# Twenty seven-product pairs instead of eighteen in a down projection, with two weight sums joined into one instruction

## The chip, the cores and the metric

The kernel runs on one core of a Trainium2 chip. The metric is the device time of one execution in microseconds (us). Three runs of the kernel before took 1113.10 to 1113.37 us, median 1113.29. One more execution was profiled; all durations and waits below come from it.

## The reference

One layer of a streaming encoder for 256 tokens of width 2048, in float32: a joint input projection, eight heads of retention beside eight heads of latent attention, an output projection, a layer norm, a feed-forward block, a second layer norm. What matters here is the feed-forward block, whose second product is the down projection:

```python
x = _layer_norm(DEEPNORM_ALPHA * x + mix, ln1_g[l], ln1_b[l])
h = jnp.square(jax.nn.relu(x @ w_up[l])) @ w_down[l]      # 256x2048 @ 2048x8192, then 256x8192 @ 8192x2048
x = _layer_norm(DEEPNORM_ALPHA * x + h, ln2_g[l], ln2_b[l])
```

## The kernel before, in words

**Precision by splitting.** TensorE multiplies in a reduced float32 (fp32r). Each operand is therefore split into a rounded high half (a cast on ScalarE, line 388) and the remainder, its low half (a subtraction on VectorE, line 389). A product is three matmuls: high by high, high by low, low by high.

**The down projection.** It has two passes (`p`), one for each half of the 2048 output columns. A pass runs over 32 pairs of 128-row blocks of `w_down`. A pair is one load of 1 MB into one of three raw buffers (`raw_wd`, DMA issued on SP's queue), and is then cut into pieces: a piece is a high and a low half of 1024 columns, in one of five rotating slots (`hi_wd`, `lo_wd`). ScalarE can write a piece only when TensorE is done with the piece that held the slot before. `ORDER` says in which order a pass takes the activation blocks; in pass 1 the first ten positions take weight pairs 28 to 31 and 22 to 27 and then 0, 1, 2 and on, so that the tile `lo_wd1_26` belongs to position 8 and `lo_wd1_0` to position 10. Before every second position a block of activations is split too (`r_split`, a cast and the subtraction of line 1011, tile `rhl`), except for the first positions of pass 1, whose blocks are still there. The last four pairs of pass 1 are kept for the end. The sums of a pass lie in PSUM banks (`d`).

**Ordinary and seven-product pairs.** An ordinary pair (`pair_products`) has two pieces and 24 matmuls of 512 columns. A seven-product pair (`seven_products`) takes the two by two blocks of the pair's product and forms them from seven block products in place of eight (Winograd's form of Strassen's scheme): 7 x 3 = 21 matmuls, into the banks `d` and four more (`s`). For that VectorE makes sums first. Of the activations there are four (`token_sums`, lines 363 to 366, 128 columns each, then a cast on ScalarE and a remainder on VectorE, line 368). Of the weight blocks b11, b12, b21, b22 there are four as well (`weight_sums`, lines 398 to 401, 512 columns each): t1 = b12 - b11, t3 = b22 - b12, then b12 becomes b22 - t1, then t4 = b21 - b12. t1 and t3 lie side by side in one tile, `t13`. Then four pieces are split, three of 1024 columns and one of 512: the two rows of the pair, `t13`, and t4 (tile `ut`). The table `SEVEN` names the positions of a pass that are seven-product pairs; 9 in each pass before. The up projection has 20 such pairs of its own, and the change doesn't touch their number. After the last seven-product pair of a pass the four extra banks are added into the result (`add_sums`), in between the pairs that follow, and at the start of pass 1 pass 0's banks are added to the residual.

**What sets the order.** The program is written out by hand; each engine runs its instructions in the order in which they are emitted. Pieces are emitted ahead of their use: after every part of a pair's matmuls, `unit()` emits up to two further pieces if the slots allow it, and the side work that waits. So VectorE's order (which sums, which low half, which split comes next) is fixed when the kernel is built, and moves when `SEVEN` moves.

**The end.** The last layer norm is written out in blocks of 512 columns. `shifted` finishes a block of the second 128 tokens on VectorE and writes it from SP's queue; one block is finished on ScalarE and written from ScalarE's queue. The last two writes are 384 and 128 columns.

Of the kernel before, what the change touches and what calls it, by code (L numbers as in the profile page):

```python
# [14 lines left out]
P = 128  # L15
# [19 lines left out]


ORDER = (tuple(range(16)), (14, 15, 11, 12, 13) + tuple(range(11)))
SEVEN = ((4, 7, 10, 12, 15, 18, 21, 24, 27), (2, 4, 7, 9, 12, 14, 17, 19, 22))


UP_PAIRS = (3, 5, 6)
UP_SEVEN = ((), (3, 5)) + 6 * (UP_PAIRS,)
# [37 lines left out]
def kernel(  # L80
# [19 lines left out]
    nc = tc.nc  # L100
# [60 lines left out]
    def raw_tile(job, name):  # L161
        job.raw = wraw.tile([P, 2048], F32, tag="raw", name=name)
        return job.raw
# [172 lines left out]
    for half in range(2):  # L336
        row = []
        for i in range(KT // 2):
            kp = (i + H // 2) % (KT // 2)
            n = i - (KT // 2 - 3)  # L340
            row.append(weights(w_out[half, kp], 2048, f"wo{half}{kp}",
                               into=staged_out(n) if half and n >= 0 else None))
# [15 lines left out]
    extra = {}  # L358
# [8 lines left out]
        nc.scalar.copy(v[:, :, 0], st)  # L367
        return lambda: nc.vector.tensor_sub(v[:, :, 1], st, v[:, :, 0].bitcast(F32))

    def weights_pair(name, load, half, sums=None, seven=False, into=None):  # L370


        job = Job(None, [], into is None or None in into)

        def shaped(t, like):
            return t if len(like.shape) == 2 else t.rearrange("p (f c) -> p f c", c=P)

        def split(i, src, n=1024):
            if into is None or into[i] is None:
                hi = wsp.tile([P, 1024], F32R, tag="hi", name=f"hi_{name}_{i}")  # L380
                lo = wsp.tile([P, 1024], F32R, tag="lo", name=f"lo_{name}_{i}")
            else:
                o = into[i] * 2048
                hi, lo = extra["sx"][:, o:o + 1024], extra["sx"][:, o + 1024:o + 2048]
            job.hi.append(hi)
            job.lo.append(lo)
            h, l = shaped(hi[:, 0:n], src), shaped(lo[:, 0:n], src)
            nc.scalar.copy(h, src)  # L388
            nc.vector.tensor_sub(l, src, h.bitcast(F32))  # L389

        def first_sums():
            job.rest = sums()

        def weight_sums():

            b11, b12, b21, b22 = (half(job, e, 4 * j, 4 * j + 4) for e in range(2) for j in range(2))
            t1, t3, t4 = (shaped(t, b11) for t in (extra["t13"][:, 0:512], extra["t13"][:, 512:], extra["t4"]))
            nc.vector.tensor_sub(t1, b12, b11)
            nc.vector.tensor_sub(t3, b22, b12)
            nc.vector.tensor_sub(b12, b22, t1)  # L400
            nc.vector.tensor_sub(t4, b21, b12)
            if sums:
                job.rest()

        job.load = lambda: load(job)
        if not seven:
            job.pieces = [lambda e=e: split(e, half(job, e, 0, 8)) for e in range(2)]
            job.loose = 0 if into is None else 2 - into.count(None)
        else:
            job.pieces = ([first_sums] if sums else []) + [weight_sums]  # L410
            job.loose = len(job.pieces)
            job.pieces += [lambda: split(0, half(job, 1, 0, 8)), lambda: split(1, half(job, 0, 0, 8)),
                           lambda: split(2, extra["t13"]), lambda: split(3, extra["t4"], 512)]
        job.free = [[False] for _ in job.pieces[job.loose:]]
        jobs.append(job)
        return job

    def up_pair(b, kp):
        def load(job):
            raw = raw_tile(job, f"raw_wu{b}_{kp}")  # L420
            nc.sync.dma_start(raw.rearrange("p (f c) -> p f c", f=8),
                              w_up[8 * b:8 * b + 8, :, kp * 256:(kp + 1) * 256].rearrange("f p c -> p f c"))

        def half(job, e, i, j):
            return job.raw.rearrange("p (f e c) -> p f e c", f=8, e=2)[:, i:j, e]

        return weights_pair(f"wu{b}_{kp}", load, half, None, kp in UP_SEVEN[b])

    def down_pair(p, pair, into=None, seven=None):
        def load(job):  # L430
            raw = raw_tile(job, f"raw_wd{p}_{pair}")
            nc.sync.dma_start(raw.rearrange("p (e c) -> p e c", e=2),
                              w_down[2 * pair:2 * pair + 2, :, p * 1024:(p + 1) * 1024].rearrange("e p c -> p e c"))

        def half(job, e, i, j):
            return job.raw[:, e * 1024 + i * P:e * 1024 + j * P]

        def sums():
            k = 2 * pair
            r0, r1 = (rr[k // 32][:, k % 32 + e] for e in range(2))  # L440
            st = spare_flat[:, seven * 512:(seven + 1) * 512].rearrange("p (i c) -> p i c", i=4)
            return token_sums(r0, r1, st, sums_of(seven))

        return weights_pair(f"wd{p}_{pair}", load, half, None if seven is None else sums, seven is not None, into)

    def sums_view(t):
        return t.rearrange("p (i h c) -> p i h c", i=4, h=2)
# [1 line left out]
    def sums_of(q):  # L449
        return sums_view(extra["sx"][:, q * 1024:(q + 1) * 1024])  # L450
# [14 lines left out]
    for p in range(2):  # L465
        for n, pair in enumerate(pairs[p]):
            if p == 0 or n < 32 - NHELD:
                j_down[p][pair] = down_pair(p, pair, None, SEVEN[p].index(n) % 2 if n in SEVEN[p] else None)
                if p == 1 and n == STAGE_AT:
                    pair = pairs[1][32 - NHELD]  # L470
                    j_down[1][pair] = down_pair(1, pair, (2, 3))
            elif n > 32 - NHELD:
                j_down[p][pair] = down_pair(p, pair, (1, None) if n == 33 - NHELD else None)
    j_down[0][pairs[0][SEVEN[0][0]]].held = True
    row_job(2, [])
# [544 lines left out]
    for i in range(2):  # L1020
        t = work.tile([P, 2048], F32R, tag="big", name=f"us{i}", bufs=2)
# [114 lines left out]
    for b in range(1, 8):  # L1136
# [3 lines left out]
        for n in range(8):  # L1140
            job = j_block[b][n]
# [15 lines left out]
    extra["sx"] = slab.tile([P, 8192], F32R, tag="slab", name="sx")  # L1157
    j_down[0][pairs[0][SEVEN[0][0]]].held = False
    st2 = [stat.tile([P, 4, 6], F32, tag=f"ln{tb}", name=f"lm{tb}", bufs=1) for tb in range(2)]
    u, v = spare_flat[:, 0:512], spare_flat[:, 512:]  # L1160
# [44 lines left out]
    for p in range(2):  # L1205
        cb = [[(acc, bank)[p](f"d{p}{tb}{j}") for j in range(2)] for tb in range(2)]
        mb = None
        for n, pair in enumerate(pairs[p][:32 if p == 0 else 32 - NHELD]):
            b = pair // 2
            if n % 2 == 0:  # L1210
# [5 lines left out]
                if p == 1 and n == STAGE_AT:  # L1216
                    r_split(ORDER[1][15], -1)
            if n in SEVEN[p]:
                if mb is None:
                    mb = [(bank, acc)[p](f"s{p}{j}") for j in range(4)]  # L1220
                seven_products(j_down[p][pair], rhls[b], pair % 2 * 2, sums_of(SEVEN[p].index(n) % 2), cb, mb,
                               n == SEVEN[p][0], n == SEVEN[p][-1])
                if n == SEVEN[p][-1]:
# [57 lines left out]
    nc.tensor.matmul(last, scaled, col(1, 2), start=False, stop=False)  # L1281
    nc.tensor.matmul(last, warm, g2[:, 1024:1536], start=False, stop=True)

    def shifted(j, a, b):
        cs = slice(j * 512 + a, j * 512 + b)
        c = xt[:, 1, cs]
        nc.vector.scalar_tensor_tensor(c, c, rss[1], b2[:, cs], op0=ALU.mult, op1=ALU.add)
        nc.sync.dma_start(out[P:2 * P, cs], c)

    centred(1, 3, cb[1][1])  # L1290
    centred(1, 0, col(1, 0))
    shifted(3, 0, 512)
    shifted(0, 0, 512)
    nc.scalar.copy(col(1, 2), last)
    nc.scalar.dma_start(out[P:2 * P, 1024:1536], col(1, 2))
    centred(1, 1, col(1, 1))
    shifted(1, 0, 384)
    shifted(1, 384, 512)


# [77 lines left out]
```

## Time and profile before

| what | us |
|---|---|
| median of three runs | 1113.29 |
| the profiled execution: its time | 1114.0 |
| the profiled execution: its span, first to last instruction | 1111.9 |
| TensorE (PE) busy | 1103.4 |
| VectorE (DVE) busy | 903.6 |
| ScalarE (ACT) busy | 611.5 |

The runs in the table are without the profiler; the profiled execution's time is 2.1 us more than its span, for what lies around it. Rows of instructions in the profile name the engine, the line of the kernel, the operation, the tile written and the tiles read, with shapes. Rows by time begin with the start and the duration in us; "x2" merges two that follow each other, and what stands in brackets is the idle time before the row and the engine that ended it. Rows of waits name who waited for whom, then the us in total, how many times, and the longest. Rows by stage give each engine's busy us in a stretch of the span. Weight loads of the array (PEld) overlap matmuls. The granted TensorE clock was 1.00 in every stage of the down projection.

### The profile page before, as it was taken

What the parts mean: (1) busy time and instruction counts of PE and PEld (TensorE: products, weight loads), DVE (VectorE), ACT (ScalarE), POOL (GpSimd) and SP (SyncE); (2) the same over time, 40 slices, a digit from 0 to 9 for tenths busy, and PEclk for the clock granted to TensorE, in tenths of its full rate; (3) what the DMA queues carried; (4) which work ended last, traced back from release to release, by engine and by line L of the source; (5) the groups of instructions that cost most, each with busy time, mean ns of one, the idle gap of its engine ahead of it and who ended that gap; (6) DMA issues with size and microseconds to landing.
All of it is one profiled execution on the core that took longest, in us unless ns stands there. A gap on an engine that the chain in (4) does not pass through costs nothing.

```text
span 1111.9 us, 13691 instructions
## 1 busy us (share of the span) xinstructions
PE 1103.4 (99%) x5196; PEld 921.7 (83%) x5196; DVE 903.6 (81%) x1253; ACT 611.5 (55%) x793; POOL 9.6 (1%) x18
## 2 busy tenths in 40 slices
PE   9999999999999999999999999999999999999997
PEld 8888888888888889888888888888888888888875
DVE  6676784666665777899998999899999998999986
ACT  4445664535453456355666656746765664566650
POOL 0000000000000000000000000000000000000000
PEclk9999999999999999999999999999999999999999
DMA  8655364444465544566656756655656665656672
GB/s 306 224 205 189 119 233 178 154 159 161 150 259 195 200 190 151 191 224 207 212 176 202 226 153 200 217 176 171 220 187 213 206 222 175 209 190 198 206 253 100
DMA packets 92561, 217.09 MB, mean 195 GB/s; under 512 B 4176, under 2 KB 62544, under 8 KB 84432
## 3 DMA queue, kind: packets, MB, share of 16 engines
q1 hardware_dynamic: 92208, 215.70, 57.5%
q8 instruction: 40, 0.66, 0.3%
q10 hardware_dynamic: 288, 0.52, 0.1%
q14 instruction: 25, 0.20, 0.1%
HBM read 214.12 MB, written 2.10 MB: 194 GB/s over the span
## 4 chain that ended last, share of the span: by engine, by line
PE 97%; DVE 1%; DMA 1%; issue 0%; ACT 0%; POOL 0%; SPq 0%; DVEq 0%
PE d L301 22%; PE u L301 18%; PE r L301 16%; PE o L301 8%; PE v L1079 5%; PE m L301 5%; PE s L1079 4%; PE u L1079 4%; PE d L1079 3%; PE up L723 2%; PE pu L723 2%; PE ut L1126 1%; PE pv L301 1%; PE up L729 1%; DMA raw_mla<-in_w_mla 1%; PE pu L729 1%
## 5 line engine op out<-in xcount | busy, mean ns | idle before, releaser
L388 ACT CAST hi_wu<-raw_wu 128x1024 fp32r<-128x1024 f32 x112 | 118.2, 1059 | 117.9 <-DVE raw_wu L400 60.4
L388 ACT CAST hi_wd<-raw_wd 128x1024 fp32r<-128x1024 f32 x125 | 130.3, 1053 | 63.6 <-PE d L301 32.8
L389 DVE TENSOR_TENSOR lo_wd<-raw_wd,hi_wd 128x1024 fp32r<-128x1024 f32 x125 | 148.6, 1219 | 18.2 <-ACT hi_wd L388 17.0
L301 PE MATMUL u<-hi_wu,x1hl 128*128 128x512 f32 x576 | 162.7, 393 | 0.0
L301 PE MATMUL d<-hi_wd,rhl 128*128 128x512 f32 x568 | 156.5, 390 | 0.0
L389 DVE TENSOR_TENSOR lo_wu<-raw_wu,hi_wu 128x1024 fp32r<-128x1024 f32 x112 | 133.2, 1219 | 22.3 <-ACT hi_wu L388 21.6
L301 PE MATMUL r<-hi_ret,xhl 128*128 128x512 f32 x512 | 147.0, 397 | 0.0
L301 PEld LDWEIGHTS d<-hi_wd,rhl 128*128 128x128 f32 x568 | 106.3, 188 | 21.9
L301 PEld LDWEIGHTS u<-hi_wu,x1hl 128*128 128x128 f32 x576 | 106.3, 188 | 21.0
L301 PEld LDWEIGHTS r<-hi_ret,xhl 128*128 128x128 f32 x512 | 93.9, 188 | 18.2
L190 DVE TENSOR_TENSOR lo_ret<-raw_ret,hi_ret 128x1024 fp32r<-128x1024 f32 x64 | 75.7, 1220 | 23.9 <-ACT hi_ret L189 23.7
L301 PE MATMUL u<-lo_wu,x1hl 128*128 128x512 f32 x288 | 89.0, 390 | 0.0
L301 PE MATMUL d<-lo_wd,rhl 128*128 128x512 f32 x284 | 87.9, 390 | 0.7 <-DVE lo_wd L389 0.7
L301 PE MATMUL r<-lo_ret,xhl 128*128 128x512 f32 x256 | 79.4, 391 | 0.0
L189 ACT CAST hi_ret<-raw_ret 128x1024 fp32r<-128x1024 f32 x64 | 64.9, 1051 | 16.3 <-PE r L301 12.2
L301 PEld LDWEIGHTS u<-lo_wu,x1hl 128*128 128x128 f32 x288 | 54.0, 188 | 11.4
L301 PEld LDWEIGHTS d<-lo_wd,rhl 128*128 128x128 f32 x284 | 53.2, 188 | 12.2 <-DVE lo_wd L389 1.1
L301 PE MATMUL o<-hi_wo,mix 128*128 128x512 f32 x208 | 57.1, 392 | 0.0
L301 PEld LDWEIGHTS r<-lo_ret,xhl 128*128 128x128 f32 x256 | 48.0, 188 | 10.4
L190 DVE TENSOR_TENSOR lo_wo<-raw_wo,hi_wo 128x1024 fp32r<-128x1024 f32 x26 | 31.2, 1222 | 19.6 <-ACT hi_wo L189 18.9
L301 PEld LDWEIGHTS o<-hi_wo,mix 128*128 128x128 f32 x208 | 38.7, 188 | 7.8
L301 PE MATMUL m<-hi_mla,xhl 128*128 128x512 f32 (+1 forms) x168 | 42.5, 363 | 0.0
(299 smaller groups left out, 1978.2 us busy)
## 6 DMA issues: line engine op xcount, KB each, us to landing
raw_wu<-in_w_up SPq DMA_DIRECT2D x64, 1024.0 KB, 5.7
raw_wd<-in_w_down SPq DMA_DIRECT2D x64, 1024.0 KB, 5.6
raw_ret<-in_w_ret SPq DMA_DIRECT2D x32, 1024.0 KB, 4.8
raw_wo<-in_w_out SPq DMA_DIRECT2D x16, 1024.0 KB, 4.8
raw_mla<-in_w_mla SPq DMA_DIRECT2D x14, 672.0 KB, 5.2
raw_qk<-in_w_qk SPq DMA_DIRECT2D x8, 640.0 KB, 3.9
row<-in_ln_rows SPq DMA_DIRECT2D x4, 1024.0 KB, 5.9
raw_uv<-in_w_uv SPq DMA_DIRECT2D x2, 1024.0 KB, 4.9
```

The lines of the kernel that those rows point to most:

```text
L189: nc.scalar.copy(hi[:, o:e], r)
L190: nc.vector.tensor_sub(lo[:, o:e], r, hi[:, o:e].bitcast(F32))
L301: nc.tensor.matmul(accs[j][:, :w], x_part, w_part[:, a:a + w], start=first and fst and i == 0, stop=last and lst and i == len(steps) - 1)
L388: nc.scalar.copy(h, src)
L389: nc.vector.tensor_sub(l, src, h.bitcast(F32))
L723: nc.tensor.matmul(pb, hi[:, a:a + P], hl[:, k0 + i], start=first and i == ks[0], stop=last and i == ks[-1])
L729: nc.tensor.matmul(pb[:, 0:S], lo[:, a:a + P], hl[:, k0 + i, 0:S], start=False, stop=last and i == ks[-1])
L1079: nc.tensor.matmul(pb, x_part, w_part, start=alone and first and fst, stop=alone and last and lst)
L1126: nc.tensor.transpose(pts[i][:, f * P:(f + 1) * P], gathered[i][:, f * P:(f + 1) * P], ident)
```

## The change

Three edits. First, `weight_sums` makes t1 and t3 in one subtraction of 1024 columns: `columns` gives the views [b12, b22] and [b11, b12] of the raw weights, and their difference fills `t13`. This holds for every seven-product pair, in the up projection too. Second, `SEVEN` names ten positions in each pass, at other places. Third, the very last write of 128 columns is issued from ScalarE's queue. What is computed stays the same but for rounding. Lines from 427 on are up to 9 further down.

```diff
-SEVEN = ((4, 7, 10, 12, 15, 18, 21, 24, 27), (2, 4, 7, 9, 12, 14, 17, 19, 22))
+SEVEN = ((4, 6, 9, 11, 14, 16, 19, 22, 24, 27), (2, 4, 6, 8, 10, 12, 14, 17, 19, 22))
...
-            t1, t3, t4 = (shaped(t, b11) for t in (extra["t13"][:, 0:512], extra["t13"][:, 512:], extra["t4"]))
-            nc.vector.tensor_sub(t1, b12, b11)
-            nc.vector.tensor_sub(t3, b22, b12)
+            t1, t4 = (shaped(t, b11) for t in (extra["t13"][:, 0:512], extra["t4"]))
+            second, first, t13 = columns(job, extra["t13"])
+            nc.vector.tensor_sub(t13, second, first)
             nc.vector.tensor_sub(b12, b22, t1)
             nc.vector.tensor_sub(t4, b21, b12)
...
+        def columns(job, t):
+            v = job.raw.rearrange("p (f e c) -> p f e c", f=8, e=2)
+            return (v[:, 4:8].rearrange("p f e c -> p e f c"), v[:, :, 0].rearrange("p (j f) c -> p j f c", j=2),
+                    t.rearrange("p (j f c) -> p j f c", j=2, c=P))
...
+        def columns(job, t):
+            return (job.raw.rearrange("p (e j c) -> p e j c", e=2, j=2)[:, :, 1],
+                    job.raw[:, 0:1024].rearrange("p (j c) -> p j c", j=2), t.rearrange("p (j c) -> p j c", j=2))
...
-    def shifted(j, a, b):
+    def shifted(j, a, b, queue=nc.sync):
...
-        nc.sync.dma_start(out[P:2 * P, cs], c)
+        queue.dma_start(out[P:2 * P, cs], c)
...
-    shifted(1, 384, 512)
+    shifted(1, 384, 512, nc.scalar)
```

On VectorE, the sums of weight pair 2 in pass 1 (position 12, a seven-product pair in both programs), before:

```order
L366 TENSOR_TENSOR xm_2766<-rr0_3643,xm_2766 128x128
L398 TENSOR_TENSOR t13_3672<-raw_wd1_2_8067 128x512
L399 TENSOR_TENSOR t13_3672<-raw_wd1_2_8067 128x512
L400 TENSOR_TENSOR raw_wd1_2_8067<-raw_wd1_2_8067,t13_3672 128x512
L401 TENSOR_TENSOR ut_3645<-raw_wd1_2_8067 128x512
L368 TENSOR_TENSOR sx_6382<-xm_2766,sx_6382 128x4x128
```

and now:

```order
L366 TENSOR_TENSOR xm_2766<-rr0_3643,xm_2766 128x128
L399 TENSOR_TENSOR t13_3672<-raw_wd1_2_8030 128x1024
L400 TENSOR_TENSOR raw_wd1_2_8030<-raw_wd1_2_8030,t13_3672 128x512
L401 TENSOR_TENSOR ut_3645<-raw_wd1_2_8030 128x512
L368 TENSOR_TENSOR sx_6362<-xm_2766,sx_6362 128x4x128
```

Lines 398 and 399 have become one instruction of 1024 columns.

On VectorE again, from position 9 to position 10 of pass 1 (`lo_wd1_27` to `lo_wd1_0`; `xm` holds the token sums, `rhl` is a split of activations). Before, position 9 is a seven-product pair and 10 an ordinary one:

```order
L389 TENSOR_TENSOR lo_wd1_27_2_8033<-t13_3672,hi_wd1_27_2_8032 128x1024
L1011 TENSOR_TENSOR rhl_8036<-rr0_3643,rhl_8036 128x4x256
L389 TENSOR_TENSOR lo_wd1_27_3_8052<-ut_3645,hi_wd1_27_3_8051 128x512
L389 TENSOR_TENSOR lo_wd1_0_0_8070<-raw_wd1_0_7981,hi_wd1_0_0_8069 128x1024
L389 TENSOR_TENSOR lo_wd1_0_1_8080<-raw_wd1_0_7981,hi_wd1_0_1_8079 128x1024
```

and now position 9 is ordinary, and 10 has sums of its own:

```order
L389 TENSOR_TENSOR lo_wd1_27_0_8014<-raw_wd1_27_7929,hi_wd1_27_0_8013 128x1024
L1020 TENSOR_TENSOR rhl_8017<-rr0_3643,rhl_8017 128x4x256
L389 TENSOR_TENSOR lo_wd1_27_1_8027<-raw_wd1_27_7929,hi_wd1_27_1_8026 128x1024
L363 TENSOR_TENSOR xm_2766<-rr0_3643 128x128
L364 TENSOR_TENSOR xm_2766<-xm_2766,rr0_3643 128x128
L365 TENSOR_TENSOR xm_2766<-rr0_3643 128x128
L366 TENSOR_TENSOR xm_2766<-rr0_3643,xm_2766 128x128
L399 TENSOR_TENSOR t13_3672<-raw_wd1_0_7945 128x1024
L400 TENSOR_TENSOR raw_wd1_0_7945<-raw_wd1_0_7945,t13_3672 128x512
L401 TENSOR_TENSOR ut_3645<-raw_wd1_0_7945 128x512
L368 TENSOR_TENSOR sx_6362<-xm_2766,sx_6362 128x4x128
L389 TENSOR_TENSOR lo_wd1_0_0_8048<-raw_wd1_0_7945,hi_wd1_0_0_8047 128x1024
```

One split of activations stands between the first low half of position 8 and that of position 10; between position 4 and 6, and 6 and 8, there is none, and between 10 and 12, and 12 and 14, one each.

More of the change, by code (lines that the diff above doesn't have):

```diff
@@ L368, in token_sums, with weights_pair @@
         return lambda: nc.vector.tensor_sub(v[:, :, 1], st, v[:, :, 0].bitcast(F32))
-    def weights_pair(name, load, half, sums=None, seven=False, into=None):
+    def weights_pair(name, load, half, columns, sums=None, seven=False, into=None):
         job = Job(None, [], into is None or None in into)
@@ L425, in half @@
             return job.raw.rearrange("p (f e c) -> p f e c", f=8, e=2)[:, i:j, e]
-        return weights_pair(f"wu{b}_{kp}", load, half, None, kp in UP_SEVEN[b])
+        def columns(job, t):
+            v = job.raw.rearrange("p (f e c) -> p f e c", f=8, e=2)
+            return (v[:, 4:8].rearrange("p f e c -> p e f c"), v[:, :, 0].rearrange("p (j f) c -> p j f c", j=2),
+                    t.rearrange("p (j f c) -> p j f c", j=2, c=P))
+        return weights_pair(f"wu{b}_{kp}", load, half, columns, None, kp in UP_SEVEN[b])
     def down_pair(p, pair, into=None, seven=None):
@@ L442, in sums @@
             return token_sums(r0, r1, st, sums_of(seven))
-        return weights_pair(f"wd{p}_{pair}", load, half, None if seven is None else sums, seven is not None, into)
+        def columns(job, t):
+            return (job.raw.rearrange("p (e j c) -> p e j c", e=2, j=2)[:, :, 1],
+                    job.raw[:, 0:1024].rearrange("p (j c) -> p j c", j=2), t.rearrange("p (j c) -> p j c", j=2))
+        return weights_pair(f"wd{p}_{pair}", load, half, columns, None if seven is None else sums, seven is not None, into)
     def sums_view(t):
```

## Prediction

> **What bounds the kernel now.** I read the page first, then the waits of TensorE (PE), then busy time by stage, then single instructions around the down projection's seven-product pairs.
>
> ```profile
> span 1111.9 us, 13691 instructions
> PE 1103.4 (99%) x5196; PEld 921.7 (83%) x5196; DVE 903.6 (81%) x1253; ACT 611.5 (55%) x793; POOL 9.6 (1%) x18
> ...
> PE last L1281 <- ACT xm L1279: 1.5, 1, 1.5
> PE m L482 <- POOL warm L479: 1.0, 1, 1.0
> PE d L301 <- DVE lo_wd L389: 0.7, 1, 0.7
> PE x1t L864 <- DVE xm L858: 0.2, 1, 0.2
> PE up L894 <- DVE x1hl L879: 0.2, 1, 0.2
> ```
>
> TensorE is busy 99% of the span, and its waits sum to 3.6 us, so each matmul taken away is worth its own time. One of these waits matters here: the 0.7 us in which PE waited for VectorE (DVE) in the down projection. By stage (busy us of PE, PEld, DVE, ACT, POOL; pass 0 of the down projection is 763 to 933, pass 1 up to 1077):
>
> ```profile
> 763.00:933.00 170.00, 170.00 (x760) 140.75 (x759) 157.61 (x200) 102.35 (x113) 0.00 (x0) 1.00 0.60 203
> 933.00:1006.00 73.00, 73.00 (x324) 60.45 (x323) 70.47 (x101) 42.34 (x47) 0.00 (x0) 1.00 0.57 187
> 1006.00:1052.00 46.00, 46.00 (x205) 38.06 (x204) 45.69 (x59) 30.39 (x35) 0.00 (x0) 1.00 0.62 206
> ```
>
> In pass 0 VectorE has 12.4 us to spare in 170. In pass 1 it has 2.5 in 73, then 0.3 in 46. VectorE makes every low half of the weights before PE can use it, so pass 1 is on the edge of a second bound, and the average of 81% hides that. A seven-product pair is cheap for PE and dear for VectorE. The change adds one to each pass, and crowds pass 1's first ones together.
>
> **The price of a pair.** PE, from the chain of waits:
>
> ```profile
> 1007.49 2.72 PE s L1079 x12
> 1010.89 10.88 PE d L301 x48
> ```
>
> 48 matmuls in 10.88 us are 0.2267 each. A seven-product pair has 21 (4.76), an ordinary one 24 (5.44). VectorE, a stretch of pass 1 where it runs without a pause (start, duration):
>
> ```profile
> 1000.49 0.28 DVE L363 TENSOR_TENSOR xm<-rr 128x128 f32<-128x128 f32 x1
> ...
> 1001.42 0.68 DVE L398 TENSOR_TENSOR t<-raw_wd 128x512 f32<-128x512 f32 x1
> 1002.02 0.68 DVE L399 TENSOR_TENSOR t<-raw_wd 128x512 f32<-128x512 f32 x1
> 1002.74 0.69 DVE L400 TENSOR_TENSOR raw_wd<-raw_wd,t 128x512 f32<-128x512 f32 x1
> ...
> 1004.68 2.36 DVE L389 TENSOR_TENSOR lo_wd<-raw_wd,hi_wd 128x1024 fp32r<-128x1024 f32 x2
> 1006.95 1.22 DVE L389 TENSOR_TENSOR lo_wd<-t,hi_wd 128x1024 fp32r<-128x1024 f32 x1
> ...
> 1008.68 1.22 DVE L389 TENSOR_TENSOR lo_wd<-raw_wd,hi_wd 128x1024 fp32r<-128x1024 f32 x1
> 1009.82 1.22 DVE L1011 TENSOR_TENSOR rhl<-rr,rhl 128x1024 fp32r<-128x1024 f32 x1
> 1010.96 1.22 DVE L389 TENSOR_TENSOR lo_wd<-raw_wd,hi_wd 128x1024 fp32r<-128x1024 f32 x1
> ```
>
> I count from start to start, because neighbours overlap. A seven-product pair costs 1000.49 to 1008.68, 8.19 us. An ordinary pair is two low halves, 1004.68 to 1006.95, 2.27. A split of activations (L1011) is 1.14. So an ordinary pair gives VectorE 3.17 us of lead over PE, a seven-product pair takes 3.43 back, a split 1.14. The lead can't be saved up: the pieces share five slots, and ScalarE waits for PE to free one:
>
> ```profile
> ACT hi_wd L388 <- PE d L301: 36.2, 20, 2.1
> ```
>
> **The two sums in one instruction.** Two 512-element instructions become one of 1024. Between starts the first takes 0.60, the second 0.72 since L400 needs its result at once: 1.32. One of 1024 takes 1.14 (1008.68 to 1009.82), and I add the same 0.12 for the dependent that follows: 1.26. It saves 0.07 us per seven-product pair (0.066 before rounding). The operands of the new one jump between column ranges, which no row of 1024 with two inputs shows; bounds are 1.14 (saves 0.18) and twice the 0.72 (loses 0.12). I take 0.07, as the strided L1011 costs no more than L389. In the up projection's 20 such pairs PE never waits for a low half (no such row in its waits), so there it is worth nothing.
>
> The Trainium skill (VectorE: DVE Perf Modes, "The TRN2 errata — SBUF-src ops pay a fixed extra latency per instruction") gives an fp32 two-tensor instruction (N+151)/0.96 ns, 157 ns saved per joined pair. The durations agree (0.68 + 0.68 against 1.22), the starts don't, since neighbours overlap; by the page six pairs of pass 1 would stall 0.5 us less in all than below, and the time would be 1115.2.
>
> **Matmuls.** Two pairs turn from 24 to 21 matmuls: 6 x 0.2267 = -1.36 us, all on the bound engine.
>
> **Pass 0.** Seven-product pairs now stand at distances of 2 or 3. Distance 2 occurs once before, at positions 10 and 12, with two splits between them, and it just held:
>
> ```profile
> 827.19 2.35 DVE L389 TENSOR_TENSOR lo_wd<-raw_wd,hi_wd 128x1024 fp32r<-128x1024 f32 x2
> ...
> 828.69 0.39 PE L1079 MATMUL d<-lo_wd,rhl 128*128 128x512 f32 x1
> ```
>
> The first low half ended at 827.19 + 1.22 = 828.41, PE read it at 828.69: a lead of 0.28. The change has four such places (4-6, 9-11, 14-16, 22-24). 4-6 and 22-24 start from full slots and end at 0.28 + 0.07. In between the lead doesn't refill. One split lies in 9-11, where it goes by 10.20 - 11.53 = -1.33; three positions with a split (6-9, 11-14) give 4.76 + 10.88 - 8.12 - 4.54 - 1.14 = +1.84; 14-16 has two splits, -2.47. From 0.35 at 6 that makes 2.19 at 9, 0.86 at 11, 2.70 at 14, 0.23 at 16. So no stall, by a hair. By the end of the pass four ordinary pairs have refilled the slots.
>
> **Pass 1.** Positions 2, 4, 6, 8, 10, 12, 14 now follow each other with one ordinary pair between. Position 4 was reached by the same work before:
>
> ```profile
> 952.82 2.35 DVE L389 TENSOR_TENSOR lo_wd<-raw_wd,hi_wd 128x1024 fp32r<-128x1024 f32 x2
> ...
> 954.49 0.39 PE L1079 MATMUL d<-lo_wd,sx 128*128 128x512 f32 x1
> 1006.17 0.39 PE L1079 MATMUL d<-lo_wd,rhl 128*128 128x512 f32 x1
> ```
>
> Lead 954.49 - 954.04 = 0.45; the two joined sums by then make it 0.59. One step of two positions is 4.76 + 5.44 = 10.20 on PE, and on VectorE 8.12 + 2.27 = 10.39 without a split, 11.53 with one. By the order of the new program there is none in the steps to 6 and 8 and one in each of those to 10, 12 and 14. The lead goes 0.59, 0.40, 0.21 (position 8), then 0.21 - 1.33 = -1.12. So PE stalls. How much lead is left at a stall shows the one that is there:
>
> ```profile
> 1071.32 3.48 DVE L389 TENSOR_TENSOR lo_wd<-raw_wd,hi_wd 128x1024 fp32r<-128x1024 f32 x3
> ...
> 1072.59 0.74 PE L301 MATMUL d<-lo_wd,rhl 128*128 128x512 f32 x2 [0.72 <-DVE lo_wd L389]
> ...
> 1075.48 0.61 PE L301 MATMUL d<-lo_wd,rhl 128*128 128x512 f32 x2
> ```
>
> The low half ended at 1072.54, PE started 0.05 later. So the stalls are 1.12 + 0.05 = 1.17 at position 10, and 1.33 each at 12 and 14: **+3.83**. Behind the waiting matmul stands all of PE's queue, so nothing hides this. ScalarE, 30.39 busy of 46, follows VectorE, and a weight load has the time of about two pairs to land, 10.2 us:
>
> ```profile
> raw_wd<-in_w_down SPq DMA_DIRECT2D x64, 1024.0 KB, 5.6
> ```
>
> Bounds: with 0.18 saved by each of six joined sums the stalls lose 0.7 (3.1); with 0.12 lost they gain 1.1, and pass 0 loses its hair at 6, 11, 16 and 24 for another 0.6 (5.5).
>
> After position 14 the spacing is as before. The lead there is 0.05 where it was 1006.17 - 1005.90 = 0.27; three joined sums give 0.2 back, and the old stall of 0.72 stays. Following that stall 12 matmuls took 1075.48 - 1072.59 = 2.89 instead of 2.72; behind the last new stall this costs 0.17, which comes back as lead at the old one. Net 0.
>
> **Last write.** It moves from SP's queue to ScalarE's:
>
> ```profile
> 1107.41 0.88 DVE L1287 SCALAR_TENSOR_TENSOR xm<-xm,lnrs,row 128x384 f32<-128x384 f32 x2
> 1107.88 0.36 ACTq L1295 DMA_DIRECT2D out<-xm  x1
> 1108.48 0.38 SPq L1288 DMA_DIRECT2D out<-xm  x1
> ```
>
> VectorE ends at 1108.29, ScalarE's queue is free at 1108.24, SP issued at 1108.48: at most 0.19 earlier, and SP's previous write may land last. I take -0.1, between 0 and -0.2.
>
> **Sum.** -1.36 + 3.83 + 0 - 0.1 = **+2.4 us**, a span of 1114.3. The profiled execution took 1114.0 us with its span of 1111.9, the three runs 1113.29 in the median; the difference goes on the median: **1115.7 us**. The bounds make it 1114.9 to 1117.5.
>
> **Rivals.**
> *The lead carries the crowd.* If the slots hold back enough, or the joined sum is much cheaper, PE never waits, and the gain comes through whole: 1113.29 - 1.36 - 0.1 = 1111.8. For it: VectorE is idle 12.4 + 2.5 + 0.3 us in the stages above, and the added work is 2 x (8.19 - 2.27) less 20 x 0.07, 10.4. Against it: most of that idle time is in pass 0, and it can't be carried. It decides if a step with a split costs VectorE less than about 10.3. Chance 0.14.
> *Pass 0 stalls too.* If the joined instruction costs as much as two, or PE needs more than 0.2 of lead, four places of pass 0 and six steps of pass 1 lose together 1.1 to 1.7 more: about 1117.2. For it: leads of 0.23 and 0.35 are near my reading error. Chance 0.20.
> *The end is shorter by more than an issue.* The closing writes take over 2 us to land (size, median us from issue):
>
> ```profile
> out<-xm ACTq DMA_DIRECT2D x1, 256.0 KB, 2.3
> out<-xm SPq DMA_DIRECT2D x1, 64.0 KB, 2.4
> ```
>
> If 64 KB on the other queue took its quarter of ScalarE's 2.3, the end would come 1.8 earlier; with the first rival 1110.0, alone 1113.9. Against it: the 64 KB took as long as the 256. Chance 0.08, most of it with the first rival's gain. The Trainium skill (DMA: Bandwidth & Descriptors, "Issuing engines are not separate DMA queues") says that another issuing engine saves only its sequencer's time, which is the 0.1 of the sum.
>
> **How the numbers follow.** The forecast (three stalls in pass 1) has 0.58, its own range is 1114.9 to 1116.6. A measurement can tell about 0.2%, 2.2 us: below 1111.1 is faster, above 1115.5 slower. The forecast lies just over that line, so I give it 0.35 slower and 0.23 same; the first rival 0.14 same; the second 0.20 slower; the third 0.03 same and 0.05 faster. Slower 0.55, same 0.40, faster 0.05. The range 1111.8 to 1117.2 leaves out the third rival's better half and the upper part of the second.
>
> **What would show it.** PE waits for `lo_wd` at positions 10, 12 and 14 of pass 1 with 1.2 to 1.3 us each, and none in pass 0; PE 1.36 us less busy; the joined L399 at 1.2 us, 1.25 to L400's start. Wrong would be: stalls under 0.5 each, a stall in pass 0, or DVE gaps while PE waits, which would mean that ScalarE or a load comes last.

## The result and the profile after

The changed kernel takes 1116.50 us in the median of nine runs (1116.05 to 1117.43) against 1113.37 for nine of the kernel before (1113.10 to 1114.81): a ratio of 1.0025, with a 95% interval of 1.0017 to 1.0034. It is slower by a quarter of a per cent. One execution of a kernel tried further down (ten pairs in pass 0) took 1224.17 us at a granted clock of 0.85, and its ratio leaves that one out. Three matmuls fewer in each of two pairs did not pay, because TensorE (PE) now waits for VectorE (DVE) at three places of pass 1.

The page of the kernel after: span, busy time by engine, and the shares of the chain that ended last.

```profile
span 1114.5 us, 13669 instructions
PE 1103.1 (99%) x5190; PEld 921.0 (83%) x5190; DVE 911.0 (82%) x1235; ACT 615.2 (55%) x799; POOL 9.6 (1%) x18
...
PE 86%; DVE 12%; issue 2%; DMA 0%; ACT 0%; POOL 0%; DVEq 0%; ACTq 0%; POOLq 0%
```

The span grew by 2.6 us. PE still reads 99% busy and VectorE 82%, one point more than before; the averages show next to nothing. The chain does: VectorE held 1% of it before, and now 12%. The waits of PE in the kernel after say where:

```profile
PE d L1088 <- DVE lo_wd L389: 3.1, 3, 1.0
...
PE d L301 <- DVE lo_wd L389: 0.6, 1, 0.6
```

The first row is new: three waits for a low half, in a seven-product pair's matmuls (line 1088; the same line was 1079 before). The second is the old stall near the end of pass 1, 0.7 before. PE's rows by time show the three places, and busy time by stage (pass 0, pass 1 up to shortly before position 14, pass 1 from there past position 22; busy us of PE, PEld, DVE, ACT and POOL) what stands behind them:

```profile
985.71 0.50 PE L1088 MATMUL d<-lo_wd,rhl 128*128 128x512 f32 x1 [1.05 <-DVE lo_wd L389]
997.24 0.50 PE L1088 MATMUL d<-lo_wd,rhl 128*128 128x512 f32 x1 [1.04 <-DVE lo_wd L389]
1008.78 0.50 PE L1088 MATMUL d<-lo_wd,rhl 128*128 128x512 f32 x1 [1.05 <-DVE lo_wd L389]
```

```profile
763.00:933.00 170.00, 170.00 (x759) 140.75 (x758) 161.80 (x203) 103.54 (x116) 0.00 (x0) 1.00 0.61 203
933.00:1006.00 73.00, 70.91 (x312) 58.00 (x312) 72.21 (x99) 41.34 (x47) 0.00 (x0) 1.00 0.56 177
1006.00:1054.60 48.60, 47.55 (x210) 39.07 (x209) 48.26 (x60) 32.65 (x38) 0.00 (x0) 1.00 0.62 210
```

Pass 0 took its tenth pair with PE busy all the time. In pass 1, 933 to 1006, it is now VectorE that has almost nothing left (72.21 of 73), and PE that idles 2.1 us in two of the waits; the third falls into the last row. The starts of the waiting matmuls are 11.53 and 11.54 us apart; a step of two positions takes PE 10.20. The step that the prediction worked out for VectorE, as the trace has it (start, duration, what is made):

```profile
984.43 2.35 DVE L389 TENSOR_TENSOR lo_wd<-raw_wd,hi_wd 128x1024 fp32r<-128x1024 f32 x2
986.70 1.22 DVE L389 TENSOR_TENSOR lo_wd<-t,hi_wd 128x1024 fp32r<-128x1024 f32 x1
987.83 0.69 DVE L389 TENSOR_TENSOR lo_wd<-ut,hi_wd 128x512 fp32r<-128x512 f32 x1
988.44 1.22 DVE L389 TENSOR_TENSOR lo_wd<-raw_wd,hi_wd 128x1024 fp32r<-128x1024 f32 x1
989.57 1.22 DVE L1020 TENSOR_TENSOR rhl<-rr,rhl 128x1024 fp32r<-128x1024 f32 x1
990.71 1.22 DVE L389 TENSOR_TENSOR lo_wd<-raw_wd,hi_wd 128x1024 fp32r<-128x1024 f32 x1
991.84 0.29 DVE L363 TENSOR_TENSOR xm<-rr 128x128 f32<-128x128 f32 x1
...
992.77 1.22 DVE L399 TENSOR_TENSOR t<-raw_wd 128x1024 f32<-128x1024 f32 x1
994.03 0.69 DVE L400 TENSOR_TENSOR raw_wd<-raw_wd,t 128x512 f32<-128x512 f32 x1
994.75 0.69 DVE L401 TENSOR_TENSOR ut<-raw_wd 128x512 f32<-128x512 f32 x1
995.37 0.68 DVE L368 TENSOR_TENSOR sx<-xm,sx 128x512 fp32r<-128x512 f32 x1
995.97 2.35 DVE L389 TENSOR_TENSOR lo_wd<-raw_wd,hi_wd 128x1024 fp32r<-128x1024 f32 x2
```

There is no bracket in these rows: VectorE does not wait for anything. From the first low half of position 10 (984.43) to that of position 12 (995.97) it needs 11.54 us. The joined sum, L399, takes 1.22 us, and L400 starts 1.26 us after it. PE's first low-half matmul starts 0.05 us after the low half (995.97 + 1.22 = 997.19, and 997.24).

What PE loses is the distance of the starts less 10.20, not the wait in the row. The wait reads 1.05 and the loss is 1.33, for two reasons: the last matmul ahead of the wait is drawn 0.39 us long where its step is 0.23, so 0.16 of the idle time is counted as busy; and the matmuls right behind a wait run a little slower (0.33 us from 985.71 to the next start, 986.04, in place of 0.23).

### The profile page after: what moved, and what is told of

Its sections match the earlier page's. It is cut to its first block, busy times and chain, and to the rows that moved or that the text cites. A ratio compares the mean times of both kernels' runs of the same rounds, so it can differ in the third digit from the quotient of the medians.

```text
span 1114.5 us, 13669 instructions
## 1 busy us (share of the span) xinstructions
PE 1103.1 (99%) x5190; PEld 921.0 (83%) x5190; DVE 911.0 (82%) x1235; ACT 615.2 (55%) x799; POOL 9.6 (1%) x18
## 4 chain that ended last, share of the span: by engine, by line
PE 86%; DVE 12%; issue 2%; DMA 0%; ACT 0%; POOL 0%; DVEq 0%; ACTq 0%; POOLq 0%
PE u L301 18%; PE r L301 16%; PE d L301 13%; PE o L301 8%; DVE lo_wd L389 6%; PE v L1088 5%; PE m L301 5%; PE u L1088 4%; PE s L1088 2%; PE d L1088 2%; PE up L732 2%; PE pu L732 2%; PE ut L1135 1%; DVE t L399 1%; PE pv L301 1%
## 5 line engine op out<-in xcount | busy, mean ns | idle before, releaser
L301 PE MATMUL d<-hi_wd,rhl 128*128 128x512 f32 x552 | 152.3, 390 | 0.0
L301 PEld LDWEIGHTS d<-hi_wd,rhl 128*128 128x128 f32 x552 | 103.3, 188 | 21.3
L301 PE MATMUL d<-lo_wd,rhl 128*128 128x512 f32 x276 | 85.5, 390 | 0.6 <-DVE lo_wd L389 0.6
L367 ACT CAST sx<-xm 128x512 fp32r<-128x512 f32 x20 | 12.4, 622 | 70.1 <-DVE xm L366 70.1
```

What stands on the lines that cost most here:

```text
L301: nc.tensor.matmul(accs[j][:, :w], x_part, w_part[:, a:a + w], start=first and fst and i == 0, stop=last and lst and i == len(steps) - 1)
```

## The experiments

Times are medians, each beside runs of the kernel before on the same chip. Ratios are against the kernel before.

### Which part costs the time: the places taken apart

Three kernels keep the joined sum and the last write, and change only `SEVEN`: the old places, ten pairs in pass 0 alone, ten in pass 1 alone (the three added lines, in this order). This and the later diffs are against the kernel after.

```diff
-SEVEN = ((4, 6, 9, 11, 14, 16, 19, 22, 24, 27), (2, 4, 6, 8, 10, 12, 14, 17, 19, 22))
+SEVEN = ((4, 7, 10, 12, 15, 18, 21, 24, 27), (2, 4, 7, 9, 12, 14, 17, 19, 22))
+SEVEN = ((4, 6, 9, 11, 14, 16, 19, 22, 24, 27), (2, 4, 7, 9, 12, 14, 17, 19, 22))
+SEVEN = ((4, 7, 10, 12, 15, 18, 21, 24, 27), (2, 4, 6, 8, 10, 12, 14, 17, 19, 22))
```

Old places:

> The change with the nine old places in each pass: only the joined sums and the last write on ScalarE's queue are left of it. Theory (the time is lost in pass 1's crowd of seven-product pairs alone): the old stall at the end of pass 1 shrinks from 0.72 to about 0.55 us by the lead that the joined sums give, nothing else moves: -0.2 us, ratio 0.9998, no other wait of PE for a low half. Rival (the joined sums or the last write cost time themselves, since the changed kernel's median rose 3.1 us and its profiled span only 2.6): +0.5 us or more, ratio 1.0005 or above.

Ten in pass 0:

> The change with its ten places in pass 0 and the nine old ones in pass 1. Theory: pass 0 holds with a least lead of 0.2 to 0.3 us, so its three matmuls come off whole: -0.68 - 0.2 = -0.9 us, ratio 0.9992, no wait of PE for a low half in pass 0. Rival (pass 0's close places cost something that the leads don't show): no gain or a loss, ratio 1.0000 or above.

Ten in pass 1:

> The change with the nine old places in pass 0 and its ten in pass 1. Theory: the three delays at positions 10, 12 and 14 (3.9 us in all) stay, one pair's 0.68 us comes off, and the stall at the end is as in the changed kernel: +3.1 us, ratio 1.0028, that is 0.7 us over the changed kernel. Rival (the stalls come of both passes together, through a lead that pass 0 had lost): fewer or shorter delays in pass 1, ratio under 1.0020.

| kernel | us | kernel before | ratio, 95% interval |
|---|---|---|---|
| old places | 1113.53 | 1114.06 | 0.9996 [0.9987, 1.0005] |
| ten in pass 0 | 1112.64 | 1114.06 | 0.9988 [0.9979, 0.9997] |
| ten in pass 1 | 1116.90 | 1114.06 | 1.0027 [1.0017, 1.0036] |

The joined sum and the last write alone change nothing that can be measured; the old stall, expected at 0.55 us, took 0.9 in the profiled execution (see The old stall below). Pass 0's tenth pair is a gain: by the starts of the passes' first low-half matmuls, pass 0 took 169.20 us (763.73 to 932.93) against 169.86 before, 0.66 less, where three matmuls are 0.68. VectorE is busy 162.56 of the stage's 170 us, and PE all through:

```profile
763.00:933.00 170.00, 170.00 (x759) 140.69 (x759) 162.56 (x205) 104.08 (x117) 0.00 (x0) 1.00 0.59 202
```

Pass 1's tenth pair is the whole loss. With ten in pass 1 alone the kernel is 2.8 us over the one before, where 3.1 was expected, and the waits are those of the kernel after:

```profile
PE d L1088 <- DVE lo_wd L389: 3.1, 3, 1.0
```

The kernel with ten pairs in pass 0 and the nine old ones in pass 1 beats both kernels, by 1.4 us against the one before; its interval ends just under 1. Not all of this is the tenth pair's: in the profiled execution, 1.4 shorter as well, 0.66 comes from pass 0 and about as much from the old stall in pass 1, which took 0.07 us and not 0.7.

One profiled span did not fit. That of the old places was 1113.1 us, 1.2 over the kernel before, although VectorE ended only 0.18 later. The closing writes explain it (size, us from issue to landing):

```profile
out<-xm ACTq DMA_DIRECT2D x1, 256.0 KB, 3.4
out<-xm SPq DMA_DIRECT2D x1, 192.0 KB, 3.7
out<-xm ACTq DMA_DIRECT2D x1, 64.0 KB, 3.6
```

In that one execution, the slowest of its eleven (1114.92), each of the three landed about 1.0 later than in the kernel after (2.3, 2.6 and 2.6). The median is not touched by it. A single profiled span of this kernel can be off by 1 us for this reason alone.

### Is it the length of VectorE's step: less work in it, and more

One kernel leaves out VectorE's four token sums (lines 363 to 366) at positions 4 to 14 of pass 1, which shortens a step; another makes the split of line 1020 twice at positions 8, 10 and 12, which lengthens it.

```diff
-    def token_sums(r0, r1, st, v):
+    def token_sums(r0, r1, st, v, old=False):
...
+        if not old:
+            nc.vector.tensor_add(st[:, 0], r0[:, P:], r1[:, P:])
...
-            return token_sums(r0, r1, st, sums_of(seven))
+            return token_sums(r0, r1, st, sums_of(seven), p == 1 and pairs[1].index(pair) in (4, 6, 8, 10, 12, 14))
```

```diff
-        nc.vector.tensor_sub(t[:, :, S:], r, t[:, :, 0:S].bitcast(F32))
+        for _ in range(1 + again):
+            nc.vector.tensor_sub(t[:, :, S:], r, t[:, :, 0:S].bitcast(F32))
...
-                    r_split(ORDER[1][i])
+                    r_split(ORDER[1][i], again=n in (8, 10, 12))
```

Sums left out:

> The changed kernel without the four token sums (lines 363 to 366) of the six seven-product pairs at positions 4 to 14 of pass 1, which use the sums of an earlier pair; those products are therefore of other sums, and all matmuls and all other instructions stay. VectorE has 0.93 us less to do per step and nothing runs on GpSimd. Theory (VectorE's work per step is the bound): the lead at position 4 is 1.5 us, capped near 2.7 behind a seven-product pair, 1.3 at 10, 0.9 at 12 and 0.5 at 14, so all three delays go: -1.36 - 0.3 = -1.7 us, ratio 0.9985. Rival (ScalarE, the slots or the loads set the delays): they stay, ratio 1.0020 or above.

Split twice:

> The changed kernel with the subtraction of the activation split (line 1020) done twice at positions 8, 10 and 12 of pass 1: one more instruction of 1.14 us on VectorE in each of the three steps that end at 10, 12 and 14. Theory: each delay grows by the whole 1.14, to 2.4, 2.5 and 2.5 us, so +3.4 on the changed kernel and +6.2 to +6.5 on the kernel before, ratio 1.0057. Rival (something else comes last in these steps, and VectorE has room): less than half of it, ratio under 1.0045.

Without the sums: 1112.24 against 1113.62, a ratio of 0.9986 [0.9977, 0.9995]. The three waits of the seven-product pairs are gone. The lead of the low half over PE at positions 4, 10, 12 and 14 was 1.54, 1.28, 0.87 and 0.47, as expected to 0.1. It still falls by 0.4 a step with a split, so even without the sums a step is longer for VectorE than for PE; the lead merely lasts to the end of the crowd. The old stall near the end stays (0.9 us).

With the split twice: 1120.59 against 1113.62, 1.0058 [1.0046, 1.0071]. PE's rows at positions 10, 12 and 14, and VectorE's row of the doubled split:

```profile
986.70 0.50 PE L1089 MATMUL d<-lo_wd,rhl 128*128 128x512 f32 x1 [2.22 <-DVE lo_wd L389]
999.50 0.50 PE L1089 MATMUL d<-lo_wd,rhl 128*128 128x512 f32 x1 [2.22 <-DVE lo_wd L389]
1012.29 0.77 PE L1089 MATMUL d<-lo_wd,rhl 128*128 128x512 f32 x1 [2.22 <-DVE lo_wd L389]
```

```profile
990.57 2.48 DVE L1021 TENSOR_TENSOR rhl<-rr,rhl 128x1024 fp32r<-128x1024 f32 x2
```

The steps became 12.80 and 12.79 us. That is 1.26 more than 11.54: the second split starts at once behind the first, and the pair of them takes 2.40 to the next start (992.97) where one takes 1.14. Three times this is 3.8; by the two ratios (1.0058 and 1.0025) the kernel is 3.7 slower than the kernel after. That the two agree so well is partly luck, since PE also lost time behind the third wait. The rows that follow it:

```profile
1012.86 0.63 PE L1089 MATMUL d<-hi_wd,rhl 128*128 128x512 f32 x1
1013.29 0.63 PE L1089 MATMUL d<-hi_wd,sx 128*128 128x512 f32 x1
```

Here the starts are 0.43 us apart and not 0.23, and the granted clock of 1012 to 1024 reads 0.86 where the kernel after has 1.00. To position 17's first low-half matmul this costs 1.6 us more than in the kernel after, of which a shorter old stall (0.2 instead of 0.6) gives 0.4 back; the profiled span is 4.6 over that of the kernel after. Up to position 14, what VectorE is given in this stretch, PE pays in full; what it is spared, PE gains until the delay is used up. The three waits are VectorE's throughput, not a slot, ScalarE or a load.

### Is it the joined sum's price

The two sums are made separately again, with the rest as in the kernel after.

```diff
-            nc.vector.tensor_sub(t13, second, first)
+            t3 = shaped(extra["t13"][:, 512:], b11)
+            nc.vector.tensor_sub(t1, b12, b11)
+            nc.vector.tensor_sub(t3, b22, b12)
```

> The changed kernel with the two weight sums in two instructions again, at its twenty places. From the first sum's start to that of line 400's instruction 1.32 us instead of 1.25. Theory: pass 0 is at the edge (0.1 us of delay at position 16), in pass 1 the lead is used up at position 8 already and the delays are 0.15, 1.39, 1.39 and 1.39 us: 0.5 to 0.6 us more in all than in the changed kernel's trace, span 1115.0 to 1115.1. If the joined sum is worth its durations' difference (0.15 us each): 1.0 us more or above.

A single execution, without an interval: 1117.49 us, span 1115.4. VectorE's rows of the sums before position 10:

```profile
981.47 0.69 DVE L400 TENSOR_TENSOR t<-raw_wd 128x512 f32<-128x512 f32 x1
982.08 0.68 DVE L401 TENSOR_TENSOR t<-raw_wd 128x512 f32<-128x512 f32 x1
982.80 0.69 DVE L402 TENSOR_TENSOR raw_wd<-raw_wd,t 128x512 f32<-128x512 f32 x1
```

The two took 1.33 from the first start to the dependent one, the joined 1.26: joining saves 0.07 per pair. PE's losses grew from 1.21, 1.33 and 1.34 to 1.41, 1.40 and 1.41. As expected, the lead was used up at position 8 already (0.05 instead of 0.18, with 0.13 lost there), and pass 0 was at its edge: at position 16 the lead was 0.05 instead of 0.20, and 0.19 was lost. From position 4 of pass 0 to position 22 of pass 1 this kernel loses 0.8 on the kernel after, but it had begun 0.3 ahead of it, so it stands 0.4 behind. That is about half of the 0.9 on the span; the other half came at the stall near the end of the pass, 1.1 instead of 0.6, which the theory did not foresee.

### Can another engine take the work

The four token sums go to GpSimd, which is idle.

```diff
-        nc.vector.tensor_add(st[:, 0], r0[:, P:], r1[:, P:])
-        nc.vector.tensor_sub(st[:, 1], st[:, 0], r0[:, 0:P])
-        nc.vector.tensor_sub(st[:, 2], r0[:, 0:P], r0[:, P:])
-        nc.vector.tensor_sub(st[:, 3], r1[:, 0:P], st[:, 1])
+        nc.gpsimd.tensor_add(st[:, 0], r0[:, P:], r1[:, P:])
+        nc.gpsimd.tensor_sub(st[:, 1], st[:, 0], r0[:, 0:P])
+        nc.gpsimd.tensor_sub(st[:, 2], r0[:, 0:P], r0[:, P:])
+        nc.gpsimd.tensor_sub(st[:, 3], r1[:, 0:P], st[:, 1])
```

> The changed kernel with the four token sums of each seven-product pair (0.93 us on VectorE) made by GpSimd, which is idle; all 20 places stay. Theory (VectorE's work per step is the bound): a step of two positions costs VectorE 9.46 us without a split and 10.60 with one, against 10.20 on PE; the lead is 2.4 us at position 4 and never under 1.5 up to 14, so the three delays go and the matmuls come off whole: -1.36 - 0.2 = -1.5 us, ratio 0.9986. Rival (the delays come from ScalarE, the slots or the loads, and VectorE only shows them): the delays stay, ratio 1.0020 or above. A second rival: GpSimd is too slow for the sums and becomes what the low halves wait for, which its row in the waits would show.

This expectation failed: 1115.70 against 1114.06, 1.0015 [1.0006, 1.0023]. Two of the three waits remain, 2.1 us in all. VectorE's rows of this kernel beside GpSimd's (POOL) of the same time show why:

```profile
983.65 2.62 DVE L389 TENSOR_TENSOR lo_wd<-raw_wd,hi_wd 128x1024 fp32r<-128x1024 f32 x2
986.20 1.48 DVE L389 TENSOR_TENSOR lo_wd<-t,hi_wd 128x1024 fp32r<-128x1024 f32 x1
987.60 0.95 DVE L389 TENSOR_TENSOR lo_wd<-ut,hi_wd 128x512 fp32r<-128x512 f32 x1
988.47 1.48 DVE L389 TENSOR_TENSOR lo_wd<-raw_wd,hi_wd 128x1024 fp32r<-128x1024 f32 x1
989.87 1.21 DVE L1020 TENSOR_TENSOR rhl<-rr,rhl 128x1024 fp32r<-128x1024 f32 x1
```

```profile
937.55 0.46 POOL L364 TENSOR_TENSOR xm<-xm,rr 128x128 f32<-128x128 f32 x1
...
983.81 1.37 POOL L363 TENSOR_TENSOR xm<-rr 128x128 f32<-128x128 f32 x1 [6.62 <-DVE sx L368]
985.26 1.33 POOL L364 TENSOR_TENSOR xm<-xm,rr 128x128 f32<-128x128 f32 x1
986.56 1.44 POOL L365 TENSOR_TENSOR xm<-rr 128x128 f32<-128x128 f32 x1
987.96 0.91 POOL L366 TENSOR_TENSOR xm<-rr,xm 128x128 f32<-128x128 f32 x1
```

And VectorE's rows beside the first of these:

```profile
937.07 0.68 DVE L814 TENSOR_TENSOR xm<-xm,d 128x512 f32<-128x512 f32 x1
937.78 0.69 DVE L817 BATCH_NORM_STATS2 lm<-xm 128x6 f32<-128x512 f32 x1
```

The same five low halves took VectorE 5.14 us in the kernel after (984.43 to 989.57) and take 6.22 here (983.65 to 989.87): 1.08 more, about 0.27 for each GpSimd instruction that runs beside them. On VectorE the four sums had taken 0.93 (991.84 to 992.77). Moving them away costs VectorE 0.15 a pair where it was to save 0.93. The steps say the same: PE's starts at 984.95, 996.60 and 1008.26 are 11.65 and 11.66 apart, 0.12 longer than in the kernel after. That one wait is gone all the same comes from the start of the pass: there GpSimd made sums while VectorE was idle, or while it ran instructions of which at most one input lies in SBUF (L814, whose other input is a PSUM bank, and L817), and took 0.46 us each. So the pass entered the crowd with a lead of 2.23 at position 4 and not 0.59.

### Number or place

Could ten pairs of pass 1 stand where they don't crowd? First they were spread over positions 2 to 24, in the spacing of the kernel before:

```diff
-SEVEN = ((4, 6, 9, 11, 14, 16, 19, 22, 24, 27), (2, 4, 6, 8, 10, 12, 14, 17, 19, 22))
+SEVEN = ((4, 6, 9, 11, 14, 16, 19, 22, 24, 27), (2, 4, 7, 9, 12, 14, 17, 19, 22, 24))
```

> The changed kernel with pass 1's ten places spread out: 2, 4, 7, 9, 12, 14, 17, 19, 22, 24, so the nine old ones and one more behind them. Is it the number of pairs in the pass or their place? If only the crowd's place counts: no delay from 2 to 22, and the whole gain but for the old stall, -1.4 us, ratio 0.9988. If the pass has no room for a tenth pair anywhere: about 3 us of delays in its last part, ratio 1.0020 or above. By adding up the lead I expect something between: it is 0.26 at position 24 and 0.1 behind it, then 0.6 us of delay, and the sums of the extra banks now fall two positions later into the end, which can't be added up as the loads set the pace there: +0.3 us, ratio 1.0003.

1122.08 against 1113.62, 1.0069 [1.0056, 1.0082], from one single wait:

```profile
PE d L1088 <- DVE sx L1020: 7.8, 1, 7.8
```

Up to position 24 the ten places cost nothing: PE waits for no low half of `w_down` in this kernel, and the lead at 24 is still 0.19, near the 0.26 that I had added up. Behind that the run answers another question than the one asked. At position 24 the split of the last activation block is already being written into the place of `sx` that holds the sums, so the pair there waits for it. It also multiplies other sums than it should, and the last step that adds up the sums of products is not reached; these two are the changed part of the computation. No seven-product pair can stand at 24 without another buffer. The places were therefore moved again, ending at 22:

```diff
-SEVEN = ((4, 6, 9, 11, 14, 16, 19, 22, 24, 27), (2, 4, 6, 8, 10, 12, 14, 17, 19, 22))
+SEVEN = ((4, 6, 9, 11, 14, 16, 19, 22, 24, 27), (2, 4, 6, 8, 11, 13, 16, 18, 20, 22))
```

> The changed kernel with pass 1's ten places moved to 2, 4, 6, 8, 11, 13, 16, 18, 20, 22; the last one stays at 22, so nothing behind it moves. The question that the spread left open: number or place? Theory (VectorE hasn't the time for a tenth pair between positions 2 and 22, wherever it stands): by adding up the lead no delay before position 18, then 1.3 us each at 20 and 22, 2.6 in all in place of 3.9; behind 22 as before: -1.36 + 2.6 = +1.3 us, ratio 1.0012. Rival (only the run of seven close places from 2 to 14 costs): no delay but the old stall, -1.4 us, ratio 0.9988.

1116.44 against 1113.89, 1.0024 [1.0015, 1.0034]: as slow as the kernel after, and slower than I expected.

```profile
PE d L1088 <- DVE lo_wd L389: 2.0, 2, 1.0
...
PE d L301 <- DVE lo_wd L389: 1.0, 1, 1.0
```

The two waits fell where the leads, added up as in the prediction, end: at positions 20 and 22 (PE's starts 1025.75, 1037.27 and 1048.80, so 1.32 and 1.33 lost). What I had wrong is the stretch behind. I had taken the pass to recover behind 22 as before; but the stall at the end of the pass cost 0.84 more than in the kernel before. The load whose landing sets this stall (see The old stall below) was issued 6.25 us behind position 22's first low-half matmul, and 5.02 behind it in the kernel before. By its own account: -1.36 + 2.65 + 0.84 = +2.1, and the span grew from 1111.9 to 1114.0. So the place decides where PE waits. Two spacings that end at 22 lose about as much as each other, and neither has room for a tenth pair. That the number alone decides is not shown: spread to 24, ten pairs cost no wait for a low half up to there, and what such a pass would do behind 24, with a buffer of its own for the sums, was not run.

## Why the prediction was right

The forecast was 1115.7 us, of the kind "slower, by three stalls in pass 1". Measured are 1116.5, near the top of the forecast's own range (1114.9 to 1116.6), and the three stalls are there. Point by point:

**Pass 0.** No stall, as forecast. The leads at positions 6, 9, 11, 14, 16 and 24 were forecast as 0.35, 2.19, 0.86, 2.70, 0.23 and 0.35; the trace has 0.34, 2.17, 0.83, 2.67, 0.20 and 0.34. The rival "pass 0 stalls too" is out by a hair, as the lead of 0.20 at 16 shows; with two sums in place of the joined one, pass 0 did lose 0.19 there.

**Pass 1.** The bookkeeping of the lead held to 0.03 us, that of the losses to 0.04:

| position | lead forecast | lead measured | lost by PE, forecast | lost, measured |
|---|---|---|---|---|
| 4 | 0.59 | 0.59 | 0 | 0 |
| 6 | 0.40 | 0.39 | 0 | 0 |
| 8 | 0.21 | 0.18 | 0 | 0 |
| 10 | 0.05 | 0.06 | 1.17 | 1.21 |
| 12 | 0.05 | 0.05 | 1.33 | 1.33 |
| 14 | 0.05 | 0.05 | 1.33 | 1.34 |

In all 3.88 where 3.83 was forecast (PE's starts at positions 8 to 14: 974.30, 985.71, 997.24, 1008.78). The rival "the lead carries the crowd" is out; the run without the token sums shows what would have made it true, about 0.9 us less VectorE work in each step.

**Behind position 14.** The forecast was that nothing more is gained or lost. At 14 the kernel stood 2.61 us behind the kernel before, at position 17 2.71, and at the last piece of pass 1 2.59. The 0.1 that slower matmuls lost behind the last wait came back at the old stall, as forecast (0.17).

**The joined sum.** Forecast 1.26 to the next start, measured 1.26; a saving of 0.07 a pair, which the run with two sums confirms (1.33). The Trainium skill (VectorE: DVE Perf Modes, "The TRN2 errata — SBUF-src ops pay a fixed extra latency per instruction") would have it 0.157; its formula fits the durations (1.22 and 0.69), but not the distance between starts, by which the work is done.

**The last write.** This term was wrong, by 0.1. The rows of VectorE's end, of the write's issue, and its landing:

```profile
1110.00 0.88 DVE L1296 SCALAR_TENSOR_TENSOR xm<-xm,lnrs,row 128x384 f32<-128x384 f32 x2
```

```profile
1110.92 0.39 ACTq L1297 DMA_DIRECT2D out<-xm  x1
```

```profile
out<-xm ACTq DMA_DIRECT2D x1, 64.0 KB, 2.6
```

It was issued 0.04 us after VectorE's end (1110.88) instead of 0.19, so the 0.15 was there; but it took 2.6 us to land instead of 2.4. From VectorE's end to the end of the span are 3.62 us, and were 3.63. The rival "the end is shorter by more than an issue" is out. The Trainium skill's rule that I had named (DMA: Bandwidth & Descriptors, "Issuing engines are not separate DMA queues") agrees: only issue time was saved, and here not even that reached the end.

**TensorE's busy time.** I had said that PE would be 1.36 us less busy; it is 0.3 less (1103.4 to 1103.1). The matmuls are gone, but of the 3.88 us that PE lost at the three places its rows show only 3.1 as waiting: the other 0.7 is drawn as busy, by the long last matmul ahead of each wait and the slower ones behind it. That leaves -0.6; the last 0.3 I can't place. The step that failed was to read the removed matmuls off the busy sum, which the stalls fill again.

**The sum.** On the span: start of pass 0 +0.07, pass 0 -0.67, pass 1 up to 14 +3.21, the rest -0.02: +2.6, forecast +2.4. The medians rose by 3.1. Of the 0.5 between them, 0.2 is that the profiled span of the kernel before, 1111.9, stood above the usual one: it was 1111.7 in the median of 32 later runs of it. The rest I can't place; that kernel's median itself went from 1113.4 to 1114.1 between sets of runs.

**The old stall.** The old stall near the end of pass 1 took anything from 0.07 to 1.1 us in kernels that differ little there: 0.7 before, 0.6 after, 0.9 with the old places, 0.07 with ten in pass 0, 1.1 with two sums; the old places and ten in pass 0 have the same pass 1. Some 13 us ahead of it VectorE waits for ScalarE's cast (2.50 us in the kernel after, 2.10 with ten in pass 0), and ScalarE for a load of weights, as ScalarE's rows of these two kernels show, in this order:

```profile
1061.26 1.05 ACT L388 CAST hi_wd<-raw_wd 128x1024 fp32r<-128x1024 f32 x1 [3.53 <-DMA raw_wd<-in_w_down]
```

```profile
1057.24 1.05 ACT L388 CAST hi_wd<-raw_wd 128x1024 fp32r<-128x1024 f32 x1 [3.29 <-DMA raw_wd<-in_w_down]
```

VectorE's low half of this cast follows, and from there, in both, VectorE works without a pause up to the low half that PE waits for. In ten of the eleven kernels here (all but the one spread to 24) the matmul that waits starts 13.9 us after this cast (1075.20 - 1061.26 in the kernel after), whether it waited 0.07 or 1.1 us. In nine of them the load ends the cast's wait; in the kernel with the split twice TensorE, which frees a slot, comes last. So this cast's start sets the old stall, and in all kernels but that one a load's landing sets the cast. Counted from position 22's first low-half matmul, the cast starts 10.87 us later in the kernel after, 10.97 before, 11.13 with the old places, 10.30 with ten in pass 0 and 11.38 with two sums. Why the load lands sooner or later stays open. It is worth up to 1 us, about as much as the better version gained, and the forecast had nothing for it but the stall of the kernel before.

## What to carry to other kernels

Where one engine feeds another, add up the feeder's work from start to start over each step of the schedule and carry the lead along, place by place; a feeder that is 82% busy over the whole kernel can be the bound for 35 us of it, and then a saving on the other engine turns into a wait. Take a change of this kind apart by place before giving it up: one half gained 0.9 us on the old places (1113.53 to 1112.64, by the medians), the other lost 3.4 (to 1116.90). And before moving work to an idle engine, time it while the busy one runs, not alone.

## What was unexpected of the hardware

**GpSimd slows VectorE, and VectorE slows GpSimd.** In the kernel with the sums on GpSimd, a 128x128 sum takes GpSimd 0.46 us while VectorE is idle or takes at most one input from SBUF. Beside VectorE's instructions with two inputs in SBUF it takes 1.33 to 1.44 (1024 columns) or 0.91 (512 columns); each of VectorE's, 1.22 or 0.69 us alone, takes 1.48 or 0.95 then. Over all 20 pairs, by groups of instructions (total busy us, mean ns of one, idle time before):

```profile
L389 DVE TENSOR_TENSOR lo_wd<-t,hi_wd 128x1024 fp32r<-128x1024 f32 x20 | 28.3, 1413 | 0.0
```

```profile
L363 POOL TENSOR_TENSOR xm<-rr 128x128 f32<-128x128 f32 x20 | 27.2, 1358 | 471.7 <-DVE sx L368 368.2 <-ACT rr L1129 62.0 <-DVE xm L1180 41.5
```

The first group's mean was 1218 ns in the kernel after. The Trainium skill (SBUF — State Buffer, "Who interferes with whom") says that a VectorE instruction with two inputs in SBUF contends with a GpSimd instruction that reads SBUF, calls the ports that the two share an exclusive lock, and says that the order of issue decides who is blocked. The trace agrees that both lose. The sizes fit with taking turns: a sum takes GpSimd's 0.46 plus most of the VectorE instruction, and ends 0.32 us behind it (988.00 against 987.68, 988.87 against 988.55). But VectorE loses only 0.26 each time, less than the 0.46, so it is not blocked for the whole of a sum; how the two share was not tested. I had not weighed this when I set the expectation for that run.

**Matmuls behind a wait can run at about half speed.** Behind the waits of 1.0 us in the kernel after, starts were 0.23 us apart again from the third matmul on, and behind the first two waits of 2.2 us in the kernel with the split twice the granted clock read 1.00. Behind its third such wait, and behind the one of 7.8 us in the kernel spread to 24, some eight matmuls started 0.43 apart, and the granted clock of the 4 us from the wait's end reads 0.57 and 0.56. So a wait can cost more than its own length; which waits do was not tested.

**The closing writes have a spread of 1 us** from one execution to another (2.6 and 3.6 us for the same 64 KB), more than the last write's move was to gain.
